# First three units' weights issued ahead of all stores; norm steps of a tile next to its product; differential values in a bank of the dense products

## The chip, the cores and the metric

One core of a Trainium2 chip runs one transformer layer in one launch. The metric is the device time of that launch in microseconds, as a median over several executions. The core has TensorE (matmuls and transposes, into eight PSUM banks), VectorE, ScalarE and GpSimd (elementwise work), and SyncE, which here issues nearly all DMAs. Each engine works through its own list of instructions in order; a semaphore releases an instruction when its inputs are there or its buffer is free. In the profile the engines are called PE (with PEld, its weight loads), DVE, ACT, POOL and SP.

## The reference

One layer, 1024 positions, width 1024, all float32. Cut to what matters:

```python
h = rmsnorm(x, g[0]);  proj = h @ w_in                      # (1024 x 1024) @ (1024 x N_IN)
# three branches read slices of proj
hm = sigmoid(mo) * head_rms(mlstm(...))                     # 4 heads x 256, in chunks
hd = rmsnorm(diff_attention(dq, dk, dv, lam), subln) * 0.2  # 8 heads, values 128 wide
hr = silu(rg) * head_rms(retention(...))                    # 4 heads x 256, in chunks
y  = gm * (hm @ w_mlstm_out) + gd * (hd @ w_diff_out) + gr * (hr @ w_ret_out)
x  = x + rmsnorm(y @ w_out, g[1])
a, u = split(rmsnorm(x, g[2]) @ w_ffn_in);  x = x + rmsnorm((silu(a) * u) @ w_ffn_out, g[3])

# diff_attention, for a block of 128 queries (its keys end at kend)
s = where(allowed, q @ k.T - slope * |t - s|, -inf)         # two score maps, c = 0, 1
p = softmax(s);  a = p[0] - lam * p[1];  o = a @ v
```

## The kernel before, in words

Every float32 product is made of three passes (mm3, line 108): each operand is split into a high and a low part, and hi·hi, hi·lo and lo·hi are added up in PSUM (lines 111 to 113). A split (line 104) is a cast on ScalarE (line 105) and a subtraction on VectorE (line 106); split weights are called wh and wl.

The large projections run as **units** (class Unit, line 287). A unit takes 256 columns of a weight in two tiles (load, line 295, issued by SyncE at line 297) and makes them with seven products instead of eight: p1 to p7 pair a role of the weights (B11, B21, T1 to T4, B22) with a role of the activations (A11, A12, A22, S1 to S4). T1 to T4 are differences of weight blocks (line 306) that are then split; S1 to S4 are sums and differences of activation blocks (left_sums, line 276, sums at line 279, then split). Each product is 12 matmuls of 128x512.

A stretch of units starts with begin (line 394), since the activations come in column by column: turned (line 249) transposes them with TensorE (line 255), and ScalarE and VectorE drain and split them (lines 262 to 271). begin works through three units at once: p1 and p2 of each while the second half of the activations is still being turned, then p5, p6, p7, p3, p4 of all three. It hands the subtractions of these three units to GpSimd (u.eng). After begin, steady (line 354) takes unit after unit. begin runs twice: at the start on the normed x (tiles x0 to x7 of 128 rows, load_x and normed), called the opening here, and before the feed-forward part on the normed x of the second half (z, from run_last), the second opening.

The three branches' cores are sequential, so dense work is woven between their steps (weave, line 1473): a core yields the worth of a step, and the weave draws dense matmuls at a given rate. For the differential core (diff_core, line 825) the dense work is the branch products and then the output projection: 63 steps for each 892 of worth. A unit of that core, of which there are 64 (8 heads x 8 query blocks), is turn (transposes of the weights, line 869), scores of the unit after next (line 843; VectorE adds the bias and takes the maximum, line 845, the scaled maximum nmx is line 849, the exponential line 850), finish of the unit before (transpose of its result hk, line 897), and values (line 879, then a square on ScalarE, a power on GpSimd and hk on VectorE, line 887). PSUM has eight banks: psum() takes one of four that the cores, the turns and some products share, psum(True) one of four for the dense products.

Branch products read the branch's output back from DRAM in load_branch (line 991), which splits it (bh, bl) beside the dense steps: beside (line 1000) advances it one step for each dense step. run_last (line 1104) is the last block of the output projection: for each of four row tiles the product, and the norm steps (norm_steps, line 1058: square and factor, scale at 1066, add at 1067, store to x2 at 1068, second square and factor, z at 1071) spread over the next tiles' products.

The order of instructions on each engine comes from a scheduler that works on the order in which this program emits them; SyncE issues in the order that comes out, and a store holds the DMAs behind it until its data is there.

## Time and profile before

| | |
|---|---|
| median of 3 runs | 2662.22 us (2660.33 to 2663.09) |
| profiled execution, its own time | 2657.28 us |
| its span, first to last instruction | 2655.5 us |
| mean granted clock of TensorE in it | 0.984 |
| TensorE busy | 2534.3 us (95%) |
| VectorE, ScalarE, GpSimd busy | 65%, 46%, 10% |

The profiled execution is one run; its times are read as starts in us from its first instruction. An engine that shows idle time waits for what the row names behind the arrow. The granted clock is 1.00 at TensorE's full 2.4 GHz and 0.50 at its lower level, 1.2 GHz; a value between is a mixture in that stretch. A busy share is a mean over stages that have different limits.

### The profile page before, as it was taken

Reading aid. Unit: us, or ns where it says so; the run is one execution under the profiler, and the core shown is the slowest. Engines: PE = TensorE matmul, PEld = TensorE weight load, DVE = VectorE, ACT = ScalarE, POOL = GpSimd, SP = SyncE. Lnnn points to the kernel's source line nnn. Section 1 sums busy time; section 2 is a strip of 40 time slices with the busy share of each in tenths; the row PEclk is TensorE's granted clock in tenths of the full one; section 3 lists DMA queues with packets and bytes.
Section 4 is the critical chain, followed back from the end, with each engine's and each line's share of the span. In section 5 each row is a group of like instructions: output and inputs, shape, how many; then the busy total and the mean of one; then the engine's idle time right before and its main releaser. Section 6 shows DMA issues by size and latency. Waiting matters only on the chain. (4 is left out here: it accounts for less than half of the span.)

```text
span 2655.5 us, 35304 instructions
## 1 busy us (share of the span) xinstructions
PE 2534.3 (95%) x12061; PEld 2062.1 (78%) x12061; DVE 1731.7 (65%) x3618; ACT 1233.6 (46%) x2500; POOL 262.8 (10%) x393
## 2 busy tenths in 40 slices
PE   5989999999999999999999989989979999999997
PEld 4778888888888888888877767768767888887885
DVE  7679778657656666556467776763457655655756
ACT  5554554454444444444455554542454333333444
POOL 3000000000000000000001111222213110110000
PEclk9999999999999999999999999999989999999999
DMA  3343445444545545444476566663523332327342
GB/s 122 90 129 114 143 135 151 129 128 135 152 127 166 155 141 159 139 128 122 135 212 165 147 182 164 170 209 124 176 83 111 103 104 91 110 93 285 104 142 80
DMA packets 402077, 368.92 MB, mean 139 GB/s; under 512 B 18957, under 2 KB 302046, under 8 KB 401898
## 3 DMA queue, kind: packets, MB, share of 16 engines
q1 hardware_dynamic: 399424, 364.45, 45.9%
q10 hardware_dynamic: 2474, 2.22, 0.3%
q8 instruction: 95, 1.56, 0.3%
q14 instruction: 84, 0.69, 0.1%
HBM read 249.92 MB, written 116.69 MB: 138 GB/s over the span
## 5 line engine op out<-in xcount | busy, mean ns | idle before, releaser
L105 ACT CAST wh<-ws 128x512 fp32r<-128x512 f32 (+1 forms) x622 | 384.9, 623 | 749.0 <-PE ps L112 561.4
L106 DVE TENSOR_TENSOR wl<-ws,wh 128x512 fp32r<-128x512 f32 (+1 forms) x622 | 455.7, 736 | 256.0 <-ACT wh L105 245.7
L306 DVE TENSOR_TENSOR ws<-ws,ws 128x512 f32<-128x512 f32 x216 | 148.7, 689 | 101.7 <-DMA ws<-in_w_in_dram 58.6
L111 PE MATMUL ps<-bh,wh 128*128 128x512 f32 x384 | 155.9, 411 | 8.2 <-ACT bh L105 8.2
L112 PE MATMUL ps<-bl,wh 128*128 128x512 f32 x384 | 156.3, 409 | 0.4 <-DVE bl L106 0.2
L113 PE MATMUL ps<-bh,wl 128*128 128x512 f32 x384 | 155.0, 405 | 0.0
L111 PE MATMUL ps<-A11h,wh 128*128 128x512 f32 x312 | 127.7, 409 | 14.6 <-ACT wh L105 12.6
L319 ACT COPY s2k<-ps 128x512 f32<-128x512 f32 x234 | 135.9, 582 | 9.4 <-PE ps L113 7.2
L111 PE MATMUL ps<-S1h,wh 128*128 128x512 f32 x312 | 127.4, 410 | 9.5 <-ACT S1h L105 8.0
L111 PE MATMUL ps<-S2h,wh 128*128 128x512 f32 x312 | 125.5, 403 | 3.6 <-ACT s2k L319 3.6
L112 PE MATMUL ps<-S1l,wh 128*128 128x512 f32 x312 | 126.0, 404 | 1.4 <-DVE S1l L106 1.4
L459 DVE TENSOR_TENSOR s2k<-ps,s2k 128x512 f32<-128x512 f32 x108 | 74.3, 688 | 78.7 <-PE ps L113 70.8
L112 PE MATMUL ps<-A11l,wh 128*128 128x512 f32 x312 | 125.6, 402 | 0.1
L111 PE MATMUL ps<-S3h,wh 128*128 128x512 f32 x312 | 125.0, 401 | 0.7 <-ACT s2k L319 0.7
L113 PE MATMUL ps<-A11h,wl 128*128 128x512 f32 x312 | 125.5, 402 | 0.1
L111 PE MATMUL ps<-S4h,wh 128*128 128x512 f32 x312 | 125.4, 402 | 0.0
L113 PE MATMUL ps<-S1h,wl 128*128 128x512 f32 x312 | 125.4, 402 | 0.0
L112 PE MATMUL ps<-wl,wh 128*128 128x512 f32 x308 | 121.3, 394 | 4.2 <-DVE wl L106 4.2
L111 PE MATMUL ps<-A12h,wh 128*128 128x512 f32 x312 | 124.8, 400 | 0.0
L111 PE MATMUL ps<-A22h,wh 128*128 128x512 f32 x312 | 124.6, 399 | 0.0
L112 PE MATMUL ps<-S2l,wh 128*128 128x512 f32 x312 | 124.2, 399 | 0.0
L112 PE MATMUL ps<-S4l,wh 128*128 128x512 f32 x312 | 124.1, 398 | 0.0
(304 smaller groups left out, 6511.2 us busy)
## 6 DMA issues: line engine op xcount, KB each, us to landing
ws<-in_w_in_dram SPq DMA_DIRECT2D x112, 512.0 KB, 4.5
ws<-in_w_ffn_in_dram SPq DMA_DIRECT2D x44, 512.0 KB, 3.9
m_dram<-s2k SPq DMA_DIRECT2D x64, 256.0 KB, 2.3
ch<-m_dram SPq DMA_DIRECT2D x32, 512.0 KB, 6.1
r_dram<-s2k SPq DMA_DIRECT2D x64, 256.0 KB, 2.3
ch<-r_dram SPq DMA_DIRECT2D x32, 512.0 KB, 5.3
qk_dram<-s2k SPq DMA_DIRECT2D x64, 256.0 KB, 3.6
dk<-qk_dram SPq DMA_DIRECT2D x64, 256.0 KB, 5.6
```

The source lines that it names most:

```text
L105: nc.scalar.copy(hi, src)
L106: nc.vector.tensor_sub(lo, src, hi.bitcast(F32))
L111: nc.tensor.matmul(ps, lh, rh, start=start, stop=False, skip_group_check=more)
L112: nc.tensor.matmul(ps, lh, rl, start=False, stop=False, skip_group_check=more)
L113: nc.tensor.matmul(ps, ll, rh, start=False, stop=stop, skip_group_check=more)
L306: self.eng.tensor_tensor(*sub[r], op=ALU.subtract)
L319: nc.scalar.copy(t, ps)
L459: nc.vector.tensor_add(part, ps, part)
```

## The change

In the opening, the loads of the first three units' weights are issued directly behind the first four x tiles, and the norms of x4 to x7 are issued after the drains of the first half's turned columns (marks). begin no longer loads the second and third unit in its midst, and all subtractions of weights run on VectorE. Each split now stands directly before its own product, unit by unit. In the differential core the result of values takes a bank of the dense products, and finish of the unit before comes behind the dense steps that the weave draws after the scores; the weave's rate goes from 63 to 60 per 892, and load_branch advances two steps for each dense step. In run_last the first two units of the feed-forward part are loaded at its start, and the norm steps of a tile follow its product at once; the second square writes its unused result into z instead of a scratch tile.

```diff
-    def norm_factor(src):
-        ss = square_sum(src, D, "x")
+    def norm_factor(src, junk=None):
+        ss = square_sum(src, D, "x", junk)
...
     def split(self, *roles):
-                    self.eng.tensor_tensor(*sub[r], op=ALU.subtract)
+                    nc.vector.tensor_sub(*sub[r])
...
     def begin(units, seven, xs, turns):
         a, b, c = units
-        for u in units:
-            u.eng = nc.gpsimd
+        for u in (b, c):
+            if u.raw[0] is None:
+                u.load(0)
+                u.load(1)
         a.p1()
         a.p2(False)
-        b.load(0)
-        b.load(1)
         b.split("B11", "B21")
         for _ in range(3):
             next(turns, None)
         b.p1()
         b.p2(False)
+        a.split("T1")
         for _ in range(2):
             next(turns, None)
-        c.load(0)
-        c.load(1)
         c.split("B11", "B21")
...
         sums = left_sums(seven, xs)
-        for u in units:
-            u.split("T1")
         next(sums)
-        for u in units:
-            u.p5(False)
-            u.split("T2")
-        next(sums)
-        for u in units:
-            u.p6()
-            u.split("T3")
...
+        for role, p in (("T1", "p5"), ("T2", "p6"), ("T3", "p7"), ("B22", "p3"), ("T4", "p4")):
+            for u in units:
+                if role != "T1" or u is not a:
+                    u.split(role)
+                getattr(u, p)(*([False] if p == "p5" else []))
+            next(sums, None)
...
         def values(u):
-            o_ps = psum()
+            o_ps = psum(True)
...
             if later is not None:
                 scores(later)
+            w = qb + 3
+            yield w
             if n > 0:
                 finish(units[n - 1])
-            w = qb + 3
-            yield w
             if n + 1 < len(units):
                 weights(units[n + 1])
             values(u)
...
-                yield from beside(steps, sides[sh], 1)
+                yield from beside(steps, sides[sh], 2)
...
         nc.sync.dma_start(x2_dram[st * P:(st + 1) * P, :], xt)
-        rstd = norm_factor(xt)
+        rstd = norm_factor(xt, t)
...
         def run_last(w):
-            before = []
-            ups[0].load(0)
-            ups[0].load(1)
+            for u in ups[:2]:
+                u.load(0)
+                u.load(1)
             for i in range(4):
                 ps = psum(True)
                 for kt in range(KT):
                     mm3(ps, yT.tile(kt, 4 + i), w[kt // 2][kt % 2], kt == 0, kt == KT - 1)
                     if kt == 3:
                         next(turns[0], None)
-                        for g in before:
-                            next(g, None)
                         yield
+                nc.scalar.copy(z[1][i][:, halfs(1)], ps)
+                for _ in norm_steps(1, i):
+                    pass
                 next(turns[0], None)
-                nc.scalar.copy(z[1][i][:, halfs(1)], ps)
-                for g in before:
-                    next(g, None)
-                before = before[-1:] + [norm_steps(1, i)]
-                next(before[-1])
                 yield
...
     load_x(4)
-    units[0].load(0)
-    units[0].load(1)
+    for u in units[:3]:
+        u.load(0)
+        u.load(1)
...
+    marks = []
+    for _ in turned(hn[:4], 0, 72, hT, hx, marks):
         pass
     for st in range(4, NT):
-        normed(st)
+        with tc.issue_after(marks[st - 2].ins):
+            normed(st)
...
-    weave(diff_core(), 63 / 892)
+    weave(diff_core(), 60 / 892)
```

The lists of instructions differ at three places; elsewhere the engines' orders are the same but for GpSimd, which loses the 24 subtractions, and VectorE, which gains them. SyncE at the opening, before (ws are weight tiles of the units, x the x tiles, m_dram<-s2k a store):

```order
L1428 DMA x_27_159<-in_x_dram 128x1024
L297 DMA ws_72_311<-in_w_in_dram 128x8x128
L297 DMA ws_73_313<-in_w_in_dram 128x8x128
L462 DMA m_dram_79<-s2k_70_294 128x512
L462 DMA m_dram_79<-s2k_86_362 128x512
L297 DMA ws_93_397<-in_w_in_dram 128x8x128
L297 DMA ws_94_399<-in_w_in_dram 128x8x128
```

After:

```order
L300 DMA ws_6_109<-in_w_in_dram 128x8x128
L300 DMA ws_7_111<-in_w_in_dram 128x8x128
L300 DMA ws_8_113<-in_w_in_dram 128x8x128
L300 DMA ws_9_115<-in_w_in_dram 128x8x128
L300 DMA ws_10_117<-in_w_in_dram 128x8x128
L1410 DMA x_16_137<-in_x_dram 128x1024
L1410 DMA x_21_147<-in_x_dram 128x1024
L1410 DMA x_26_157<-in_x_dram 128x1024
L1410 DMA x_31_167<-in_x_dram 128x1024
L451 DMA m_dram_79<-s2k_74_302 128x512
```

The two loads of the third unit stood behind two stores; all six now stand ahead of x4 to x7, and the stores behind these.

TensorE in the differential core, before, at the unit of the first head that has five key blocks (843 scores, 897 finish, 879 values, 111 to 113 dense; x4 is four matmuls):

```order
L843 MATMUL ps_3039_13508<-dk_2874_12925,dq_2873_12924 128x384
L843 MATMUL ps_3039_13508<-dk_2875_12926,dq_2873_12924 128x384
L843 MATMUL ps_3041_13515<-dk_2874_12925,dq_2873_12924 128x384
L843 MATMUL ps_3041_13515<-dk_2875_12926,dq_2873_12924 128x384
L897 MATMUL ps_3043_13522<-ident_66,hk_3027_13468 128x128
L879 MATMUL ps_3046_13530<-dv_2876_12933,s2k_3032_13498 128x128 x4
L879 MATMUL ps_3046_13530<-dv_2876_12933,s2k_3034_13502 128x128
L111 MATMUL ps_3053_13548<-bh_2883_12971,wh_2926_13127 128x512
L112 MATMUL ps_3053_13548<-bl_2884_12972,wh_2926_13127 128x512
```

After (line numbers fall by 11 there: 832 scores, 886 finish, 868 values):

```order
L832 MATMUL ps_3041_13501<-dk_2874_12925,dq_2873_12924 128x384
L832 MATMUL ps_3041_13501<-dk_2875_12926,dq_2873_12924 128x384
L111 MATMUL ps_3018_13432<-bh_2948_13194,wh_2907_13070 128x512
L112 MATMUL ps_3018_13432<-bl_2949_13195,wh_2907_13070 128x512
...
L112 MATMUL ps_3018_13432<-bl_2953_13205,wh_2907_13070 128x512
L113 MATMUL ps_3018_13432<-bh_2952_13204,wl_2908_13071 128x512
L886 MATMUL ps_3043_13522<-ident_66,hk_3027_13468 128x128
L868 MATMUL ps_3046_13530<-dv_2876_12933,s2k_3032_13484 128x128 x4
L868 MATMUL ps_3046_13530<-dv_2876_12933,s2k_3034_13488 128x128
```

finish stood right behind the scores, with values after it and the dense matmuls last; the twelve dense matmuls now stand between the scores and finish. Over the whole core 434 dense matmuls of the branches and the output projection are left for after it, where 360 were.

SyncE at the second opening, before (x2_dram<-xr are the last tiles' stores, ws from in_w_ffn_in_dram the third unit's loads):

```order
L1063 DMA xr_4834_19464<-in_x_dram 128x1024
L1068 DMA x2_dram_83<-xr_4809_19353 128x1024
L1068 DMA x2_dram_83<-xr_4824_19418 128x1024
L1068 DMA x2_dram_83<-xr_4834_19464 128x1024
L297 DMA ws_4871_19607<-in_w_ffn_in_dram 128x8x128
L297 DMA ws_4872_19609<-in_w_ffn_in_dram 128x8x128
```

After:

```order
L1052 DMA xr_4829_19461<-in_x_dram 128x1024
L1057 DMA x2_dram_83<-xr_4805_19344 128x1024
L300 DMA ws_4841_19488<-in_w_ffn_in_dram 128x8x128
L300 DMA ws_4842_19490<-in_w_ffn_in_dram 128x8x128
L1057 DMA x2_dram_83<-xr_4819_19408 128x1024
L1057 DMA x2_dram_83<-xr_4829_19461 128x1024
```

The loads of the third unit moved ahead of the stores of the last two tiles.

## Rows read from the trace of the kernel before

**Rows 1.** Page, part 1: busy us (share of the span) x instructions.

```profile
PE 2534.3 (95%) x12061; PEld 2062.1 (78%) x12061; DVE 1731.7 (65%) x3618; ACT 1233.6 (46%) x2500; POOL 262.8 (10%) x393
```

**Rows 2.** Windows, opening: stretch and its us, busy time (x instructions) by engine, clock, DMA.

```profile
0.00:25.00 25.00, 10.78 (x35) 7.47 (x36) 12.87 (x27) 15.44 (x27) 6.26 (x14) 1.00 0.81 259
...
25.00:75.00 50.00, 35.93 (x144) 27.49 (x143) 40.89 (x42) 25.33 (x40) 17.85 (x13) 0.80 0.13 37
75.00:100.00 25.00, 25.00 (x109) 20.12 (x108) 18.20 (x25) 15.00 (x22) 0.88 (x2) 1.00 0.42 116
```

**Rows 3.** Waits of TensorE, 0 to 110 us: waited for, us in total, times, longest.

```profile
PE ps L111 <- ACT wh L105: 7.3, 1, 7.3
PE ps L111 <- ACT S1h L105: 4.6, 1, 4.6
...
PE ps L111 <- DVE s2k L488: 1.5, 1, 1.5
```

**Rows 4.** Timeline of SyncE, 0 to 60 us: start, us, what it issues.

```profile
8.03 4.74 SPq L1428 DMA_DIRECT2D x<-in_x_dram  x4
...
32.96 8.03 SPq L462 DMA_DIRECT2D m_dram<-s2k  x2
41.04 1.17 SPq L297 DMA_DIRECT2D ws<-in_w_in_dram  x2
```

**Rows 5.** Timeline of VectorE, 46 to 68 us: start, us, operation.

```profile
60.95 2.28 DVE L279 TENSOR_TENSOR hx<-hx,hx 128x1024 f32<-128x1024 f32 x1
...
64.84 1.21 DVE L279 TENSOR_TENSOR hx<-hx,hx 128x1024 f32<-128x1024 f32 x1
```

**Rows 6.** Timeline of GpSimd, 30 to 62 us.

```profile
52.92 4.48 POOL L306 TENSOR_TENSOR ws<-ws 128x512 f32<-128x512 f32 x2
```

**Rows 7.** Groups by shape, VectorE, 0 to 110 us: x count | busy us, mean ns | idle before.

```profile
L106 DVE TENSOR_TENSOR wl<-ws,wh 128x512 fp32r<-128x512 f32 x25 | 21.3, 876 | 2.2 <-ACT wh L105 2.2
L279 DVE TENSOR_TENSOR hx<-hx,hx 128x1024 f32<-128x1024 f32 x8 | 12.9, 1609 | 0.5 <-ACT hx L262 0.4
...
L306 DVE TENSOR_TENSOR ws<-ws,ws 128x512 f32<-128x512 f32 x3 | 2.1, 689 | 2.3 <-DMA ws<-in_w_in_dram 2.2
```

**Rows 8.** Windows, differential stage.

```profile
1376.00:1756.00 380.00, 352.40 (x1997) 285.23 (x1996) 280.97 (x976) 193.62 (x542) 56.04 (x76) 1.00 0.63 166
```

**Rows 9.** Waits of TensorE, 1376 to 1790 us.

```profile
PE ps L897 <- DVE hk L887: 7.0, 7, 2.1
PE ps L111 <- ACT bh L105: 6.8, 4, 3.8
PE ps L843 <- DVE hk L887: 5.6, 11, 0.9
PE ps L897 <- DVE nmx L849: 4.9, 8, 1.1
```

**Rows 10.** Line 843, 1376 to 1756 us: idle ahead of it until (us, times).

```profile
  DVE hk L887: 18.1, 28
```

**Rows 11.** Windows, second opening.

```profile
1965.00:2012.00 47.00, 30.46 (x110) 22.17 (x109) 35.68 (x33) 25.09 (x40) 20.61 (x13) 0.78 0.15 45
2012.00:2040.00 28.00, 28.00 (x121) 22.34 (x120) 20.71 (x29) 12.29 (x20) 0.00 (x0) 1.00 0.55 175
```

**Rows 12.** Waits of TensorE, 1900 to 2015 us.

```profile
PE ps L255 <- ACT z L1071: 8.6, 4, 3.8
PE ps L111 <- ACT wh L105: 5.3, 1, 5.3
PE ps L111 <- ACT S1h L105: 3.4, 1, 3.4
```

**Rows 13.** Timeline of SyncE, 1940 to 1992 us.

```profile
1957.43 16.25 SPq L1068 DMA_DIRECT2D x_dram<-xr  x3
1973.77 1.47 SPq L297 DMA_DIRECT2D ws<-in_w_ffn_in_dram  x2
```

**Rows 14.** Page, part 6: DMA issues x count, KB each, median us from issue to landing.

```profile
ws<-in_w_ffn_in_dram SPq DMA_DIRECT2D x44, 512.0 KB, 3.9
```

More of the change, by code (lines that the diff above doesn't have):

```diff
@@ L208, in rsqrt, with square_sum @@
         nc.gpsimd.tensor_tensor(dst, t, expo[:, 0:1], op=ALU.pow)
-    def square_sum(src, n, tag):
-        junk = small([P, n], "junk", BF16 if n > HALF else F32, bufs=1)
+    def square_sum(src, n, tag, junk=None):
+        if junk is None:
+            junk = small([P, n], "junk", BF16 if n > HALF else F32, bufs=1)
         ss = small([P, 1], tag + "s", bufs=4)
@@ L247, in drop, with turned @@
                 self.parts.pop((role, i))
-    def turned(src, sh, g, seven, xs):
+    def turned(src, sh, g, seven, xs, marks=None):
         for kt in range(KT) if sh == 0 else (4, 5, 0, 1, 6, 7, 2, 3):
@@ L264, in turned @@
                 h, l = seven.slot(role, q)
-                nc.scalar.activation(h, ps, AF.Copy, scale=col)
+                done = nc.scalar.activation(h, ps, AF.Copy, scale=col)
+                if marks is not None:
+                    marks.append(done)
                 if kt % 2:
@@ L292, in __init__ @@
             self.seven, self.src, self.cols, self.evac, self.own = seven, w, cols, evac, own
-            self.w, self.raw, self.eng = {}, [None, None], nc.vector
+            self.w, self.raw = {}, [None, None]
         def load(self, u):
@@ L420, in begin @@
         sums = left_sums(seven, xs)
-        for u in units:
-            u.split("T1")
         next(sums)
-        for u in units:
-            u.p5(False)
-            u.split("T2")
-        next(sums)
-        for u in units:
-            u.p6()
-            u.split("T3")
-        next(sums)
-        for u in units:
-            u.p7()
-            u.split("B22")
-        next(sums)
-        for u in units:
-            u.p3()
-            u.split("T4")
-        for u in units:
-            u.p4()
+        for role, p in (("T1", "p5"), ("T2", "p6"), ("T3", "p7"), ("B22", "p3"), ("T4", "p4")):
[4 more added lines that the diff above has]
+            next(sums, None)
     def total(ps, part):
@@ L1128, in run_last @@
             ups[0].split("B11", "B21")
-            for _ in range(2):
-                for g in before:
-                    next(g, None)
         out = [Block([cols_of(w_out, ch * HALF, HALF, kp * 2, 2)], run_of(sh, ch, kp))
@@ L1457, in trunk @@
     units[0].split("B11", "B21")
-    for _ in turned(hn[:4], 0, 72, hT, hx):
+    marks = []
+    for _ in turned(hn[:4], 0, 72, hT, hx, marks):
         pass
     for st in range(4, NT):
-        normed(st)
+        with tc.issue_after(marks[st - 2].ins):
+            normed(st)
     begin(units[:3], hT, hx, turned(hn[4:], 1, 72, hT, hx))
```

## The prediction

> **What bounds the kernel now.** The page's first part comes first: TensorE is busy 2534.3 us, 95% of the span of 2655.5 us [rows 1]. So a gain can only come from the 121 us in which it does nothing, and from stretches at its lower clock; the next views say where these lie. The windows, the table of waits and the timelines put most of them into three places, and the change touches just these: the opening, the differential stage and the second opening.
>
> Opening. From 25 to 75 us TensorE ends 144 instructions at a granted clock of 0.80, and from 75 to 100 us, with everything in place, 109 in 25 us at 1.00 [rows 2]. At that pace (4.36 per us) the 144 would take 33.0 us, so 17.0 us are lost. The table of waits up to 110 us names them [rows 3]: 7.3 us for a split of the weights (line 105), 4.6 us for the split of S1, 1.5 us for a sum drained from PSUM; the other 3.6 us are mostly what the lower clock costs after each stop. The first wait has a plain cause in SyncE's timeline [rows 4]: the loads of the third unit are issued at 41.04 us because they stand behind two stores that SyncE holds for 8.03 us and that wait for results. The second is VectorE's: sums of activations (line 279, 128x1024) take 2.28 us while GpSimd works on its subtractions (4.48 us for two), and 1.21 us once it is done [rows 5, 6].
>
> Differential stage. From 1376 to 1756 us TensorE is busy 352.40 of 380 us, so 27.6 us are idle, and VectorE is busy 280.97 us, 74% [rows 8]. The waits there [rows 9]: 7.0 + 5.6 us for hk (line 887), 4.9 us for nmx (line 849), together 17.5 us, and 6.8 us for the split of a branch on which the dense matmuls work (bh).
>
> Second opening. From 1965 to 2012 us TensorE ends 110 instructions at clock 0.78, and 121 in the 28 us behind that [rows 11]; at 4.32 per us the 110 would take 25.5 us, so 21.5 us are lost. The waits: 8.6 us for z (line 1071) in four, the longest 3.8 us, 5.3 us for a weight split, 3.4 us for S1h [rows 12]. SyncE again holds stores ahead of the third unit's loads, 16.25 us for three, and issues the loads at 1973.77 us [rows 13].
>
> **Part by part.** Opening (A). The six weight tiles now stand ahead of x4 to x7 and of all stores. The 7.3 us wait goes whole: the third unit's loads are issued where those of x4 were, from 8.03 us instead of 41.04 us [rows 4], long before TensorE can come to them. Moving the four x tiles behind four more weight tiles costs them 4 x 0.52 MB; at the 259 GB/s of the first window [rows 2] that is 8.1 us. What hides it: the products on A11 and A12 of three units, 72 matmuls or 16.5 us at the pace of [rows 2], need no x4 to x7. But the program has three turned columns of x4 to x7 in front of the second unit's products and TensorE runs in order, so part of the 8.1 us can show. The twelve subtractions cost VectorE 12 x 0.689 = 8.3 us [rows 7]; in return its operations no longer lengthen: 25 weight remainders at a mean of 876 ns against the 689 ns of a subtraction of the same shape give 4.7 us, eight sums at 1609 ns against 1210 ns 3.2 us [rows 5, 7]. That is 7.9 against 8.3 us: VectorE's load stays as it is, and what counts is that the splits now stand each beside its product, so S1's no longer queue behind three units' T1. I take 7.3 us, 4.6 us less 2.4 us (a sum at 1.21 us and a remainder of the same size still stand ahead of the first S1 product), 1.5 us, and 2 of the 3.6 us of lower clock: **13 us**. Ends: 17.0 us if all goes; 17.0 - 8.1 - 4.6 = 4 us if x4 to x7 are late in full and the S1 wait stays.
>
> The Trainium skill speaks of the two engines' ports (SBUF — State Buffer, in "SBUF: two separate sides"): an operation of VectorE with two SBUF inputs and one of GpSimd share a port pair as an exclusive lock, and the later one waits for the whole of the other. The sum at 2.28 us beside GpSimd and 1.21 us alone agrees as to the sign; by the rule VectorE could win back up to GpSimd's whole 17.85 us of work from 25 to 75 us [rows 2], and A would lie at its upper end of 17 us; by the rows it wins 7.9 us, and the sum goes by that.
>
> Differential stage (B). Four things move. (1) The results of the values' matmuls (line 879) leave the four banks that scores, turns and finish share for the four of the dense products; a bank is held until hk (line 887) is written, and the scores waited for just that: 18.1 us of weight-load idle before line 843, 28 times, until hk [rows 10]. (2) finish (line 897), which waited for hk and nmx behind the scores, now has about 12 dense matmuls ahead of it, 2.8 us. (3) The dense rate falls from 63 to 60 per 892, and in the order 434 dense matmuls are left for after the stage, where 360 were. They are not lost time: 74 matmuls at 0.229 us are 17 us that leave the stage and come back behind it at full pace. (4) load_branch is fed two steps at a time, so that the splits that TensorE waited 6.8 us for come earlier. Price: 17.5 us of hk and nmx, 4 of the 6.8 us, together 21.5 us. Against this stands VectorE: its 281 us of work would fall into 380 - 17 - 21 = 342 us, 82%, and it works through the units in order, so some of the wait moves to its other results. I discount to **15 us**. Ends: 27.6 us (no idle left) and 0 (all of it returns as waits for VectorE). The bank of the dense products is what hides (1): if it isn't free, see the rival below.
>
> Second opening (C). In SyncE's new order the third unit's loads stand in front of the last two stores, so they are issued behind the store of the second tile, not behind that of the fourth. The norm steps of a tile follow its own product. The weight wait (5.3 us) goes; of the 3.4 us for S1h I take 2.5, as some of VectorE's work stays ahead of it; the rest of the loss, 21.5 - 5.3 - 3.4 - 8.6 = 4.2 us, is mostly lower clock behind these two waits, and goes with them. The waits for z stay in the sum: the chain of the last tile (square, factor, scale, add, square, factor, copy) has no work of TensorE's left to cover it. 5.3 + 2.5 + 4.2 = **12 us**. Ends: 5 us (the weight wait alone) and 16 us (the z wait of the last tile also goes). One thing is added: ScalarE's cast of the third unit's first weights now stands before the squares of the last two tiles; if that load is late, the norm chain waits behind it. Such a load lands 3.9 us after its issue [rows 14], and it is issued while the second tile's norm still runs, so I price it at nothing; the lower end covers it.
>
> Sum: 13 + 15 + 12 = 40 us. The profiled execution took 2657.28 us, 4.94 us less than the median of 2662.22 us. 2657.28 - 40 + 4.94 = 2622 us.
>
> **Rivals.** R1, slower: the banks of the dense products run out. Results of values are held there for the whole chain to hk, and a dense product must wait once in each of 64 units. The wait per unit is priced by the same wait for the same chain before, 18.1 / 28 = 0.65 us [rows 10]: 64 x 0.65 = 41.4 us. With B at 0 and A and C giving 25 us the time is 2657.28 + 41.4 - 25 + 4.94 = 2679 us. It turns the sum over from 25 / 64 = 0.39 us per unit. Against it: a dense product of 24 matmuls spans two units, so about three banks are taken in two units and one comes round after four, or 2.7 units of 380 / 64 = 5.9 us, 16 us; the chain to hk is a few us.
>
> R2: VectorE is the bound of the differential stage, and B gives 0; A and C give 25 us: 2637 us. For it: 74% already, and the waits named are nearly all for VectorE's results [rows 9]. Against it: they are waits for a chain's end, not for a full queue, since VectorE idles 99 of 380 us.
>
> R3: the openings give only their lower ends, 4 + 5 us, with B at 15: 2657.28 - 24 + 4.94 = 2638 us. The mechanism: x4 to x7 come 8.1 us late and VectorE, with 8.3 us more to do in each opening where it is busy 40.89 of 50 us [rows 2], becomes what S1 waits for. The Trainium skill has a rule that points this way (Perfetto Trace Analysis, "Optimizing Scalar/DVE Operations"): where VectorE is saturated, giving work to ScalarE or even GpSimd may help; the change does the reverse. The same sentence warns that between GpSimd and VectorE it may not, since they share a port; the lengthening in [rows 5, 7] bears out the warning rather than the rule.
>
> R4: nothing moves. The order shows that the loads, the splits and finish do move, so this would need an unseen cost of about 40 us.
>
> **How the numbers follow.** The forecast, 2622 us with its own range of 2608 to 2632, has 0.57; R2 0.20, R3 0.13, R1 0.05, R4 0.05. The forecast's upper ends (A 17, B 27.6, C 16) reach to 2602, all at once unlikely; R2 and R3 end near 2638, and both at once at about 2653. A range of 2604 to 2645 leaves out R1, R4 and a tenth of the rest. A measurement can tell about 0.2%, 5 us, from no change: faster by more 0.90, within 0.05, slower by more 0.05.
>
> **What would show it.** A: no wait for a weight split before 60 us, no subtractions on GpSimd, line 279 at 1.21 us throughout, and at most 5 us lost between 25 and 75 us against the pace behind it. If R3: a wait for the turned columns of x4 to x7, or for S1h, of 4 us or more. B: waits for hk at lines 843 and 897 nearly gone, idle of the stage below 15 us; if R2, the idle stays near 27 us under other VectorE names; if R1, waits of line 111 for hk. C: the third unit's loads issued between the stores of the second and third tile, no wait for wh, and the lower clock gone behind the last wait for z. If the dense matmuls that leave the stage don't run at full pace behind it, B is wrong in its third step.

## The result, and the profile after

| | before | after |
|---|---|---|
| median of 4 runs | 2662.18 us | 2634.03 us (2631.39 to 2637.07) |
| after over before | | 0.9896, 95% interval 0.9878 to 0.9913 |
| profiled execution, its own time | 2657.28 us | 2631.63 us |
| its span | 2655.5 us | 2629.8 us |
| mean granted clock | 0.984 | 0.987 |

The change makes the kernel 28 us faster by the medians, 25.7 us by the two profiled executions. The forecast was 2622 us, in a range of 2604 to 2645. The first part of the page, to be set beside [rows 1]; TensorE's instructions are the same 12061:

```profile
PE 2523.2 (96%) x12061; PEld 2066.2 (79%) x12061; DVE 1730.2 (66%) x3642; ACT 1237.4 (47%) x2500; POOL 221.3 (8%) x369
```

TensorE is busy 11 us less for the same work, which fits its higher mean clock, and idle 15 us less. Where that comes from is read by stages. The first matmul of the fourth unit, the first one that steady makes, starts in the timelines of before and after at

```profile
107.46 0.39 PE L111 MATMUL ps<-A11h,wh 128*128 128x512 f32 x1
```

```profile
94.53 0.40 PE L111 MATMUL ps<-A11h,wh 128*128 128x512 f32 x1
```

so the opening gave 12.9 us. The stage of the branch products (bh), which holds the whole differential core, is read from the first and last start of its 384 matmuls of line 111, first before, then after:

```profile
L111 PE MATMUL ps<-bh,wh x384: 388/394/796, 1357.1 to 1857.1; 128*128 128x512 f32 x192
```

```profile
L111 PE MATMUL ps<-bh,wh x384: 387/394/774, 1344.2 to 1847.2; 128*128 128x512 f32 x192
```

It takes 500.0 us before and 503.0 after: the differential stage gave nothing, it took 3 us. From its end to the first matmul of the fourth feed-forward unit,

```profile
2045.05 0.39 PE L111 MATMUL ps<-A11h,wh 128*128 128x512 f32 x1
```

```profile
2019.43 0.39 PE L111 MATMUL ps<-A11h,wh 128*128 128x512 f32 x1
```

it is 187.9 us before and 172.2 after, 15.7 us gained. (Of that, the stretch up to the first A11 product loses 1.8 us, and the second opening gains 17.5 us.) 12.9 - 2.9 + 15.7 = 25.7 us is the difference of the spans, 2655.5 - 2629.8; elsewhere nothing moved by more than 0.1 us.

**Opening.** Windows, waits of TensorE up to 110 us, and SyncE's timeline, in the columns of [rows 2 to 4]:

```profile
25.00:75.00 50.00, 45.92 (x211) 36.44 (x212) 46.09 (x64) 39.94 (x61) 2.59 (x6) 1.00 0.07 28
75.00:100.00 25.00, 25.00 (x109) 20.15 (x108) 21.68 (x38) 13.99 (x21) 1.08 (x3) 1.00 0.56 159
```

```profile
PE ps L256 <- DVE hx L273: 3.3, 1, 3.3
PE ps L111 <- ACT A11h L266: 3.2, 1, 3.2
...
PE ps L111 <- ACT S1h L105: 1.7, 1, 1.7
PE ps L112 <- DVE S1l L106: 1.7, 1, 1.7
```

```profile
6.53 10.22 SPq L300 DMA_DIRECT2D ws<-in_w_in_dram  x6
16.80 3.10 SPq L1410 DMA_DIRECT2D x<-in_x_dram  x4
35.24 10.08 SPq L451 DMA_DIRECT2D m_dram<-s2k  x2
```

From 25 to 75 us TensorE now ends 211 instructions instead of 144. The wait for the third unit's weights is gone; its loads are issued within 6.53 to 16.75 us, and x4 to x7 from 16.80 us, 8.8 us later than before. That lateness hardly shows: TensorE's waits for x and its norm (xv) in the first 110 us are 3.9 us, before they were 3.2. What grew is the wait for a drain of turned columns (hx, line 273), 3.3 us where it was 1.0 (line 270); it ends at 23.61 us, ahead of this window. VectorE's timeline has its cause:

```profile
19.30 0.69 DVE L309 TENSOR_TENSOR ws<-ws,ws 128x512 f32<-128x512 f32 x1
19.91 0.69 DVE L309 TENSOR_TENSOR ws<-ws 128x512 f32<-128x512 f32 x1
20.63 0.69 DVE L309 TENSOR_TENSOR ws<-ws,ws 128x512 f32<-128x512 f32 x1
22.20 0.69 DVE L309 TENSOR_TENSOR ws<-ws,ws 128x512 f32<-128x512 f32 x1 [0.88 <-DMA ws<-in_w_in_dram]
22.81 0.74 DVE L273 TENSOR_SCALAR hx<-ps,pcol 128x512 f32<-128x512 f32 x1
```

Four subtractions of weights (309), one of which waits 0.88 us for its load, stand ahead of VectorE's first drain of turned columns, so that TensorE can't turn the next ones. Of S1's waits 1.7 us for S1h and 1.7 us for S1l are left. The sums at line 279 (now 282) take 1.22 us throughout the opening.

**Differential stage.** Waits of TensorE in the whole stage, 1344 to 1847 us (line 832 is 843 of before, 858 is 869, 886 is 897, 876 is 887, 838 is 849, 834 is 845):

```profile
PE ps L886 <- DVE mx L834: 8.1, 4, 5.3
PE ps L858 <- DVE mx L834: 5.8, 4, 2.2
PE ps L858 <- DVE sb L848: 4.5, 3, 2.0
PE ps L886 <- DVE hk L876: 4.2, 5, 1.2
...
PE ps L886 <- DVE nmx L838: 2.5, 5, 0.8
...
PE ps L111 <- ACT bh L105: 0.2, 1, 0.2
```

The waits that the change was aimed at did fall: hk and nmx from 17.5 us [rows 9] to 6.7, bh from 8.2 in the whole stage (6.8 in the window of [rows 9]) to 0.2. In their place stand 13.9 us for mx in finish and turn, where there was none, and 4.5 us for the weights (sb). All waits of TensorE in the stage, added up over this view, are 32.8 us in 41 waits before, the longest 3.8 us, and 38.7 us in 36 waits after, the longest 5.3.

Such a wait, in VectorE's and TensorE's timelines:

```profile
1596.27 0.17 DVE L845 RECIPROCAL rec<-sm 128x2 f32<-128x2 f32 x1 [0.83 <-ACT s2k L839]
1599.15 0.69 DVE L1012 TENSOR_TENSOR s2k<-ps,s2k 128x512 f32<-128x512 f32 x1 [2.72 <-DMA s2k<-gate]
...
1600.12 1.39 DVE L848 SCALAR_TENSOR_TENSOR s2k<-s2k,rat,s2k 128x128 f32<-128x128 f32 x1
...
1602.30 0.41 DVE L876 TENSOR_SCALAR hk<-ps,dfac,rec 128x128 f32<-128x128 f32 x1 [0.73 <-POOL dfac L208]
1602.63 0.68 DVE L834 CUSTOM_DVE_ANT_0 sb<-ps,ndist 128x512 f32<-128x512 f32 x1
```

```profile
1595.96 2.09 PE L832 MATMUL ps<-dk,dq 128*128 128x512 f32 x8
1603.38 0.48 PE L886 MATMUL ps<-ident,hk 128*128 128x128 f32 x1 [5.33 <-DVE mx L834]
```

The eight score matmuls fill the shared banks from 1595.96 us. finish (886) needs one of these banks, and VectorE frees the first with the maximum (834) at 1602.63 us. Before it, VectorE has stood 2.72 us at the product with a gate (1012) for that gate's DMA, 0.73 us for the power of GpSimd, and done the weights of the next unit. It works in order, so a wait on one of its inputs delays all that stands behind. TensorE loses 5.33 us there.

The clock has a part in it too. Over 380 us of the core it was 1.00 before [rows 8] and 0.96 after (row at e_dve_chain). The windows around the wait above, and of the stretch behind the core:

```profile
1598.00:1612.00 14.00, 8.67 (x35) 7.46 (x35) 10.55 (x34) 6.17 (x16) 2.36 (x3) 0.76 0.36 104
1743.00:1848.00 105.00, 103.92 (x447) 82.75 (x446) 47.01 (x74) 30.87 (x57) 27.93 (x20) 1.00 0.58 192
```

By the trace's clock records TensorE runs at 1.2 GHz for 17.0 us of the stage before and for 30.6 us after, and in the trace after, these stretches lie at waits of TensorE of 1.8 to 5.3 us. In the opening, 7 us at the lower level (clock 0.86 in 25 us, see e_after_again) cost 12 matmuls, 2.8 us, so 0.4 us for each. At that price the 13.6 us more are an estimated 5 us, an upper one, since a core that waits for other engines loses less.

**Second opening.** Windows, waits of TensorE from 1885 to 1995 us, and SyncE's timeline, to set beside [rows 11 to 13]:

```profile
1965.00:1987.00 22.00, 18.42 (x79) 13.93 (x78) 19.26 (x23) 15.77 (x26) 0.00 (x0) 0.92 0.00 1
1987.00:2015.00 28.00, 28.00 (x121) 22.44 (x120) 25.96 (x37) 13.09 (x21) 0.00 (x0) 1.00 0.51 161
```

```profile
PE ps L256 <- ACT z L1060: 4.9, 4, 2.9
PE ps L111 <- ACT S1h L105: 2.4, 1, 2.4
...
PE ps L112 <- DVE S1l L106: 0.5, 1, 0.5
```

```profile
1949.13 0.33 SPq L1057 DMA_DIRECT2D x_dram<-xr  x1
1949.55 1.48 SPq L300 DMA_DIRECT2D ws<-in_w_ffn_in_dram  x2
1955.88 6.03 SPq L1057 DMA_DIRECT2D x_dram<-xr  x2
```

The third unit's loads are issued at 1949.55 us, ahead of the last two stores, and no wait for wh is left. The waits for z fell from 8.6 to 4.9 us, those for S1h from 3.4 to 2.4 us. The lower clock is not wholly gone, 0.92 from 1965 to 1987 us, where it was 0.78 from 1965 to 2012 [rows 11].

### The profile page after: what moved, and what is told of

It reads as the page before. It is cut to its first block, busy times and chain, and to the rows that moved or that the text cites. A ratio compares the mean times of both kernels' runs of the same rounds, so it can differ in the third digit from the quotient of the medians.

```text
span 2629.8 us, 35268 instructions
## 1 busy us (share of the span) xinstructions
PE 2523.2 (96%) x12061; PEld 2066.2 (79%) x12061; DVE 1730.2 (66%) x3642; ACT 1237.4 (47%) x2500; POOL 221.3 (8%) x369
## 4 chain that ended last, share of the span: by engine, by line
PE 75%; DVE 6%; issue 5%; DMA 2%; ACT 2%; POOL 1%; SPq 0%; DVEq 0%; POOLq 0%; ACTq 0%
PE ps L112 23%; PE ps L113 23%; PE ps L111 23%; PE ps L832 2%; PE ps L868 2%; PE ps L684 1%; PE ps L643 1%; DMA s2k<-branch 1%; PE ps L858 1%; POOL dfac L208 1%; DVE wl L106 1%; DVE sb L834 1%; PE ps L691 0%; DMA dk<-qk_dram 0%; POOL xr L208 0%
## 5 line engine op out<-in xcount | busy, mean ns | idle before, releaser
L106 DVE TENSOR_TENSOR wl<-ws,wh 128x512 fp32r<-128x512 f32 (+1 forms) x622 | 447.9, 723 | 245.6 <-ACT wh L105 238.6
L309 DVE TENSOR_TENSOR ws<-ws,ws 128x512 f32<-128x512 f32 x234 | 161.0, 690 | 99.9 <-DMA ws<-in_w_in_dram 55.2
```

The lines of the kernel that those rows point to most:

```text
L106: nc.vector.tensor_sub(lo, src, hi.bitcast(F32))
L309: nc.vector.tensor_sub(*sub[r])
```

## The experiments

Each is compared with runs of the kernel before on the same chip; the ratio of the changed kernel is 0.9896 (0.9878 to 0.9913), and 0.9906 (0.9891 to 0.9921) when it was run again. "The stage" is the stretch of the branch products as read above, first to last start. Two traces of the changed kernel give 503.0 and 500.4 us for it, and before and e2_openings_only, with one order of instructions there, 500.0 and 497.5: 3 us is what one trace can't tell. In the first pair the clock accounts for it (30.6 and 23.8 us at 1.2 GHz in the stage, 2.7 us at the price above), in the second it doesn't (17.0 us in both).

**e1_diff_only**: the kernel before with the differential edits alone.

```diff
-            o_ps = psum()
+            o_ps = psum(True)
-            if n > 0:
-                finish(units[n - 1])
             w = qb + 3
             yield w
+            if n > 0:
+                finish(units[n - 1])
-                yield from beside(steps, sides[sh], 1)
+                yield from beside(steps, sides[sh], 2)
-    weave(diff_core(), 63 / 892)
+    weave(diff_core(), 60 / 892)
```

> The kernel before with only the four edits of the differential stage (bank of the dense products, finish behind the yield, 60 per 892, two steps of load_branch). Theory F (the forecast): waits for hk go and nothing takes their place, 15 us faster than before, about 2647 us. Theory T (from the trace of after): the core runs at the pace of its own chain through VectorE, ScalarE and GpSimd, the moved dense matmuls cost their time behind it; 3 us slower than before, 2660 to 2668 us.

Measured: 2658.56 us, 1.0007 of before (0.9997 to 1.0017), the stage 500.9 us. The four edits together are worth nothing; the 15 us of the forecast are refuted, and the 3 us of loss in the traces lie within what a trace can't tell. The core, from the first to the last start of the values' matmuls, takes 376.7 us, 383.4 in the kernel before, with 442 instead of 367 matmuls of the branch products left behind it.

**e2_openings_only**: the changed kernel with those edits undone (the diff above, the other way).

> The changed kernel with the differential stage as before: only the two openings are changed. Theory F: 25 us faster than before, 2637 us, so slower than the changed kernel (2634 us) by 3 us or more. Theory T: the openings gave all (12.9 us up to the first steady unit, about 16 us in the second opening), and the differential edits cost 3 us: 2631 us, as fast as the changed kernel or a little faster.

Measured: 2627.29 us, 0.9884 (0.9865 to 0.9904), the stage 497.5 us. The openings give the whole gain, 30 us on this chip. Its interval overlaps with that of the changed kernel, so whether the differential edits cost anything isn't settled.

**e_bank_m**: the bank alone undone.

```diff
-            o_ps = psum(True)
+            o_ps = psum()
```

> The changed kernel with the result of values in one of the four shared banks again; finish stays behind the yield. Theory F: scores wait for hk again, 28 times some 0.65 us, so 10 to 18 us slower than the changed kernel, 2644 to 2652 us. Theory T: the bank isn't what sets the core's pace, and the scheduler leaves 384 dense matmuls behind the core instead of 442; 2625 to 2638 us.

Measured: 2633.18 us, 0.9903 (0.9882 to 0.9925), the stage 501.7 us. The scores do wait for hk again (10.3 us in 11 waits), the waits of finish for mx are gone, and the time is the same: the edit moves waits and wins nothing. The order changes with it: 384 matmuls of the branch products are left behind the core where the changed kernel leaves 442, so 58 more (13.3 us at 0.229) run in it, and the core takes 381.0 us instead of 377.0 to 378.8. What the bank would do at one order isn't shown.

**e_finish_early**: finish alone back ahead of the yield.

```diff
+            if n > 0:
+                finish(units[n - 1])
             w = qb + 3
             yield w
-            if n > 0:
-                finish(units[n - 1])
```

> The changed kernel with finish ahead of the yield again, right behind the scores; bank of the dense products, 60 per 892 and two steps of load_branch stay. The forecast: finish waits for hk and nmx again, 11.9 us before, so about 8 us slower than the changed kernel, 2642 us. Theory D and T: no more than 3 us either way, 2631 to 2637 us.

Measured: 2636.52 us, 0.9935 (0.9916 to 0.9953), the stage 505.6 us. It is 2 to 10 us worse than the changed kernel, by medians and by ratios, though the two weren't run side by side, and 2 us worse than e_dve_more, which ran on the same chip and whose additions fall ahead of the stage (2634.78 us, the stage 501.2). The intervals overlap: whether finish's place is worth the 8 us that the forecast had for it isn't settled.

**e_rate50**: fewer dense matmuls in the core.

```diff
-    weave(diff_core(), 60 / 892)
+    weave(diff_core(), 50 / 892)
```

> The changed kernel with 50 instead of 60 dense steps per 892 in the differential core: 562 instead of 442 dense matmuls are left behind the core, 120 x 0.229 = 27.5 us. Theory F (each dense matmul in the core costs its time): no change, 2634 us, the core 27 us shorter. Theory T: the core keeps its length of 382 us from its first turn to its last values, and the time rises by up to 27 us, 2650 to 2661 us.

Measured: 2644.12 us, 0.9947 (0.9928 to 0.9966), the stage 509.0 us, which lies between the two theories. First to last start of the values' matmuls, in the changed kernel and here:

```profile
L868 PE MATMUL ps<-dv,s2k x576: 270/275/423, 1364.1 to 1742.9; 128*128 128x128 f32 x192
```

```profile
L868 PE MATMUL ps<-dv,s2k x576: 270/275/422, 1369.7 to 1726.6; 128*128 128x128 f32 x192
```

The core goes from 378.8 to 356.9 us, so 22 of the 27.5 us of dense work that left it are saved there and some 6 are not. By the ratios the whole time is 11 to 14 us longer; the stage has 6 to 9 of that. The core has no fixed length; with less dense work around it, TensorE waits more (44.5 us in the stage by the sum of its waits). Rates over 61 per 892 would draw products of the differential branch before it is written; they were not tried.

Three runs ask what the waits hang on: VectorE's work, or the time that a unit's chain takes from engine to engine.

**e_copy_act**: work taken off VectorE.

```diff
-                (nc.scalar.copy if g == 0 else nc.vector.tensor_copy)(at[:, :n * P], ps[:, :n * P])
+                nc.scalar.copy(at[:, :n * P], ps[:, :n * P])
```

> The changed kernel with the second copy of each turn moved from VectorE to ScalarE (32 copies of up to 0.68 us, at most 22 us less for VectorE, some 18 us more for ScalarE). Theory D (VectorE's own work with its waits in order sets the pace of the differential core): the core shortens by 10 to 20 us, 2614 to 2624 us. Theory T (the latency of the chain through all engines sets it): no gain, 2630 to 2638 us.

Measured: 2637.5 us, 0.9939 (0.9924 to 0.9954), the stage 506.4 us. The window of the core:

```profile
1364.00:1749.00 385.00, 345.85 (x1957) 292.43 (x1955) 272.57 (x951) 205.47 (x580) 55.46 (x75) 0.96 0.60 158
```

VectorE is busy some 9 us less in the stage than in the changed kernel (333.1 against 342.2), and the stage doesn't get shorter. ScalarE is busy 9 us more, so this run alone doesn't clear VectorE.

**e_dve_more**: work added to VectorE, first try.

```diff
             v = diff_qk[hd]["v"]
+            scr = small([P, 2 * P], "scr", bufs=1)
+            nc.vector.tensor_add(scr, ndist[:, :2 * P], ndist[:, 2 * P:4 * P])
```

> The changed kernel with one more VectorE addition of 128x256 in each of the 64 units, on constants, used by nothing: some 0.37 us each, 24 us in all. Theory D: the core gets longer by 15 us or more, 2648 to 2658 us. Theory T: VectorE's 99 us of idle time takes it in, 2632 to 2640 us.

Measured: 2634.78 us, 0.9929 (0.9914 to 0.9943). The row of the added tile says why this tells nothing:

```profile
L867 DVE TENSOR_TENSOR scr<-ndist x64: 416/424/429, 1236.8 to 1292.6; 128x256 f32<-128x256 f32 x64
```

The additions read constants, so the scheduler put all 64 ahead of the core (their starts run from 1236.8 to 1292.6 us). They have to read data of their unit:

**e_dve_chain**: the same, on the unit's turned weights.

```diff
+            wide = min(qb + 1, 2) * P
+            scr = small([P, 2 * P], "scr", bufs=1)
+            nc.vector.tensor_add(scr[:, :wide], u["at"][0][:, :wide], ndist[:, :wide])
             r1 = u["rec"][:, 0:1]
```

> The changed kernel with one more VectorE addition of 128x256 in each unit, this time on the unit's own turned weights, so that it can't run before the core: some 0.42 us each, 26 us in all. Theory D (VectorE's work sets the core's pace): 15 us or more slower than the changed kernel. Theory T (the latency of the chain sets it, VectorE has 99 us of idle time): at most 8 us slower.

Measured: 2632.02 us, 0.9909 (0.9892 to 0.9925), against 0.9906 of the changed kernel on the same chip, the stage 500.0 against 500.4 us. The windows of the core in this run and in the changed kernel:

```profile
1364.00:1743.00 379.00, 341.08 (x1956) 287.10 (x1955) 299.06 (x1048) 197.91 (x552) 54.32 (x75) 0.98 0.60 161
```

```profile
1363.00:1743.00 380.00, 344.83 (x1948) 291.75 (x1947) 281.12 (x976) 195.52 (x546) 53.28 (x75) 0.96 0.61 158
```

VectorE is busy 299.06 of 379 us instead of 281.12 of 380, and nothing gets longer. VectorE's waits for the sums of the softmax (line 845) shrink from 30.7 to 18.2 us, which is where the additions found room. VectorE's work isn't the bound.

**e_no_pow**: the chain from values to hk without GpSimd's power. The kernel leaves out the inverse root: the factor stays the mean square plus epsilon.

```diff
-            rsqrt(fac, ss, 1.0 / P, "d")
+            nc.vector.tensor_scalar(fac, ss, 1.0 / P, EPS, op0=ALU.mult, op1=ALU.add)
```

> The changed kernel without GpSimd's power in the chain from values to hk (the factor is left as the mean square plus epsilon, so that the result differs). It takes GpSimd, 0.55 us and two hand-overs out of each unit's chain; VectorE waits 24.8 us in the core for that power, in 44 units. Theory D: VectorE wins these 24.8 us back in part, 8 to 20 us faster, 2614 to 2626 us. Theory F (a wait that goes is taken by the next one, because four shared banks turn with the units): at most 5 us.

Measured: 2618.98 us, 0.9868 (0.9853 to 0.9883).

```profile
L111 PE MATMUL ps<-bh,wh x384: 387/397/774, 1347.2 to 1836.2; 128*128 128x512 f32 x192
```

The stage takes 489.0 us, 11 to 14 less; the whole time is 7 to 10 us less by the ratios, and 16 less than that of e_dve_more on the same chip. By the traces all but 12 of TensorE's 12061 instructions stand in the changed kernel's order, and its clock in the stage is that of e_after_again (23.8 us at 1.2 GHz in both). What is gone is in each unit one hand-over (a result passed from engine to engine, where the receiver waits for it) to GpSimd and one back, with the power's 0.55 us. VectorE's busy time stays (342.8 against 342.2 us in the stage), so it isn't that the two engines disturb each other less. The waits for hk shrink to 2.8 us and the sum of all waits to 29.3 us. This is more than the 5 us at most that theory F allowed: a wait that goes isn't always taken over by the next. It lies where theory D had it, which gave the gain to VectorE's waits in order. This run can't tell these waits from the length of the chain; e_fold, where they stay, points to the chain, with the reserve made there.

**e_fold**: a step less in the same chain, for the same result by arithmetic, on top of e2_openings_only.

```diff
             nc.vector.reciprocal(u["rec"], sm)
+            u["eps"] = small([P, 1], "deps", bufs=4)
+            nc.vector.tensor_scalar(u["eps"], sm[:, 0:1], sm[:, 0:1], EPS, op0=ALU.mult, op1=ALU.mult)
...
-            nc.vector.tensor_scalar(ss, ss, r1, r1, op0=ALU.mult, op1=ALU.mult)
-            fac = small([P, 1], "dfac", bufs=4)
-            rsqrt(fac, ss, 1.0 / P, "d")
+            fac, t = small([P, 1], "dfac", bufs=4), small([P, 1], "dv", bufs=4)
+            nc.vector.tensor_scalar(t, ss, 1.0 / P, u["eps"], op0=ALU.mult, op1=ALU.add)
+            nc.gpsimd.tensor_tensor(fac, t, expo[:, 0:1], op=ALU.pow)
...
-            nc.vector.tensor_scalar(hn[:, :P], o_ps[:, :P], fac, r1, op0=ALU.mult, op1=ALU.mult)
+            nc.vector.tensor_scalar(hn[:, :P], o_ps[:, :P], fac, None, op0=ALU.mult)
```

> Only the two openings changed, the differential stage as before, and one VectorE step taken out of the chain from values to hk: epsilon is multiplied by the squared sum of the softmax ahead of time, so that the scaling of the square needs one step instead of two and hk one factor. Same result. Theory T: the power's 0.55 us and two hand-overs were worth 14 us of the stage, so one step of 0.15 us and its hand-over is worth 3 to 8 us against the openings alone (0.9884 of before): 0.9855 to 0.9873. Theory D: nothing, the number of VectorE steps is the same.

Measured: 2617.6 us, 0.9851 (0.9837 to 0.9866); the changed kernel on the same chip 2632.55 us.

```profile
L111 PE MATMUL ps<-bh,wh x384: 388/397/796, 1344.9 to 1830.7; 128*128 128x512 f32 x192
```

The stage takes 485.8 us against 497.5 for e2_openings_only, and the sum of TensorE's waits in it goes from 30.0 to 24.0 us. This version beats both kernels, the changed one by 15 us. The gain is larger than forecast. VectorE waits for the power as before (27.5 us in 47 waits, 26.6 in 46 in e2_openings_only), so it isn't that wait that was saved. But the scheduler also moved about a thousand of the stage's 2454 instructions on TensorE, and only 6.8 us of the stage are at 1.2 GHz instead of 17.0, which is 4 us at the price above; how much of the gain is the step and how much the order and the clock stays open.

**e_pool_subs**: the 24 subtractions of weights on GpSimd again.

```diff
-                    nc.vector.tensor_sub(*sub[r])
+                    self.eng.tensor_tensor(*sub[r], op=ALU.subtract)
...
+        for u in units:
+            u.eng = nc.gpsimd
```

> The changed kernel with the 24 subtractions of the openings on GpSimd again; loads, order of emission and norm steps stay as changed. If the subtractions matter as the forecast has it (waits for S1h and lengthened sums return in both openings), 5 to 12 us slower than the changed kernel. If the loads alone made the gain, at most 3 us slower.

Measured: 2635.06 us, 0.9914 (0.9899 to 0.9928) against 0.9906, 2 to 3 us slower, with intervals that overlap. The trace shows more in one place. The stretch from the first feed-forward product to the fourth unit is 75.5 us instead of 70.0; the opening is as long as in the changed kernel, within what its clock does (below). Waits of TensorE at the second opening, and the sums (282) in the first (ns, least, median, most):

```profile
PE ps L112 <- DVE S1l L106: 2.6, 1, 2.6
PE ps L111 <- ACT S1h L105: 2.4, 1, 2.4
PE ps L112 <- DVE S2l L106: 1.9, 2, 1.7
```

```profile
L282 DVE TENSOR_TENSOR hx<-hx,hx x8: 1209/1213/2203, 41.7 to 69.2; 128x1024 f32<-128x1024 f32 x8
```

S1l and S2l, VectorE's remainders, are waited for 4.5 us, and a sum beside GpSimd takes up to 2203 ns where none took over 1225 in the changed kernel's first opening. The lock of the Trainium skill (SBUF — State Buffer, "SBUF: two separate sides") agrees in sign again; the Trainium skill's advice to unload a busy VectorE onto GpSimd (Perfetto Trace Analysis, "Optimizing Scalar/DVE Operations") isn't borne out here, its warning is. So the engine of the subtractions counts for some 5 us in the second opening and for nothing that can be told in the first. The rest of the gain of both openings belongs to the loads' place, the order of the splits and the place of the norm steps together; no run parts these.

**e_after_again**: the changed kernel.

> The changed kernel itself, for a comparison on one chip with the three runs beside it: 0.988 to 0.991 of the kernel before. If its four runs differ by about 5 us again, the opening's stretch of lower clock after the two waits for S1 (there in three of the traces so far, not in that of the changed kernel) should be what differs.

Measured: 2632.55 us, 0.9906, four runs within 4 us. The windows of the opening in the changed kernel's two traces and in that of e_rate50, which has the same opening:

```profile
50.00:75.00 25.00, 22.84 (x97) 18.14 (x98) 24.48 (x29) 18.32 (x25) 0.00 (x0) 1.00 0.06 22
```

```profile
50.00:75.00 25.00, 21.91 (x87) 17.34 (x88) 23.34 (x28) 17.84 (x25) 0.00 (x0) 0.93 0.03 11
```

```profile
50.00:75.00 25.00, 22.41 (x85) 17.71 (x86) 22.60 (x26) 16.88 (x24) 0.00 (x0) 0.86 0.03 11
```

Same instructions, same waits (1.7 us each for S1h and S1l), and a granted clock of 1.00, 0.93 and 0.86 in this stretch, with 97, 87 and 85 instructions ended. In eleven traces with this opening the fourth unit starts at 94.5 to 98.7 us, and the earliest is the one with clock 1.00. That this is the spread of the changed kernel's four runs (2631.4 to 2637.1) is likely, but only profiled runs show it.

## Why the prediction was right, and where not

**Right:** the sign, the range, the two openings as the places. **A** (13 us, measured 12.9 in the trace, 9 to 13 over the traces with this opening): the weight wait went whole, as it was priced, S1's waits fell to 3.4 us where 2.4 were left in the sum, and the loss from 25 to 75 us, 50 - 211 / 4.36 = 1.6 us, is below the 5 us that were named as the sign. The late x tiles, bounded with 8.1 us, cost next to nothing; the wait for hx, VectorE's subtractions ahead of a drain, wasn't in the sum. So the step on the subtractions failed in its place, not in its total: they cost in the first turned columns, which the forecast didn't look at, and with them on GpSimd (e_pool_subs) the first opening is as short.

**C** was too small: 12 us forecast, 17.5 measured, above the upper end of 16. The step that failed is "the waits for z stay in the sum": they fell from 8.6 to 4.9 us. The chain of the last tile did have cover: with its weights there early, the third unit's first products start at 1962.31 us (before, at 1986.82 us, behind the last wait for z), while the last z is still to be made (1963.57 us). The norm steps, each behind its own product, also finish earlier: from the first feed-forward product to the start of the last z it is 14.1 us, before 17.8. Which of the two won how much isn't parted by a run. The other terms came as priced.

**B** failed: 15 us forecast, 0 measured (e1_diff_only 1.0007). Three steps of it were wrong. First, the waits of (1), (2) and (4) were taken as time to be won. Of the 17.5 us for hk and nmx, which were to go whole, 10.8 went; of those for bh, 8 went where 4 were priced; and 18.4 us came back for mx and sb, so that the sum rose from 32.8 to 38.7 us. The banks, the scores, finish and turn form one loop through TensorE, VectorE, ScalarE and GpSimd, and a wait taken from one of its members turned up at the next; that it is the loop that does this is argued from the order of the instructions. The bank in particular, with the order that comes with it, is worth nothing (e_bank_m).

Second, step (3): 75 matmuls of dense work left the core, 17 us, and the core got shorter by 5 to 7 us only (383.4 us before, 378.8 and 377.0 in the two traces of the changed kernel, 376.7 in e1_diff_only). The sign that was named for this, dense work that doesn't run at full pace behind the stage, didn't come: from 1743 to 1848 us TensorE is busy 103.92 of 105 us at clock 1.00. The loss is inside the core, where TensorE is idle 35.2 of 380 us instead of 27.6. Of a further 27.5 us, 22 are saved (e_rate50).

Third, the clock, which the forecast left at 1.00 in the core, fell to 0.96 with the longer waits, an estimated 5 us of the stage at most.

The lower end, 0, and the time of rival R2, 2637 us, had B right as a number. R2's sign came too, idle time under other VectorE names (mx, sb), but not its reason: with 18 us more of VectorE's work in the core nothing got longer (e_dve_chain). What did move the stage is a shorter chain in each unit: without the power and its two hand-overs, 64 times, the stage is 11 to 14 us shorter (e_no_pow), and a VectorE step less seems to be of the same kind (e_fold).

**Rivals.** R1 didn't come: TensorE's dense matmuls wait for no bank in the stage. Its price of 0.65 us was read from idle time of the weight loads, which overlap with matmuls; TensorE's own waits there were 5.6 us in 11 [rows 9]. R3's second half came in a small size (3.3 us for hx, 3.4 for S1h and S1l), its first, the late x tiles, did not.

The sum was 13 + 15 + 12 = 40 us; measured, stage by stage, 12.9 - 2.9 + 17.5 - 1.8 = 25.7. The time lies 12 us above the forecast and 3 us from R2's. That it is within the range owes to A, which was right, to the room that the range left for a B of nothing, and to luck: C's excess, for a reason that the forecast had excluded, made up a third of B.

## What to carry to other kernels

A wait for a load that SyncE issues late, behind a store, is time to be won, and moving the load wins it whole. Waits inside a loop of several engines need not be: before adding them up, ask who takes over when one goes, and try to shorten the chain itself, a hand-over or a step in each round, since that is what moved this stage. Look at the granted clock of the new trace as well: a like sum of waits in fewer and longer pieces came here with a lower clock. To test whether an engine's load is the bound, add work to it that reads data of the same round, or the scheduler will put it elsewhere.

## What the runs showed of the hardware

In the opening, the same two short waits of TensorE (1.7 us each for S1h and S1l) came with a granted clock of 1.00 in one trace of the changed kernel and 0.93 in another over 50 to 75 us, and by 0.86 in e_rate50, whose opening is the same; 1.00 against 0.86 was worth some 3 us. A wait as short as that may or may not cost TensorE its clock.

GpSimd's subtractions lengthened VectorE's sums beside them, from 1.21 to as much as 2.20 us (e_pool_subs), and 18 us of additions on VectorE, in the midst of the core, cost nothing (e_dve_chain): there, its busy share of 74 to 79% was no sign of a bound.
